# Ordering the first addition onto a chained weight chunk behind the low part of the chunk ahead, in a two-layer hybrid encoder on one core

## The chip, the core and the metric

The program runs on one core of a Trainium2 chip. TensorE multiplies matrices, VectorE and ScalarE do elementwise work, GpSimd does a little of it and issues transfers that add into their destination, SyncE issues the other transfers, and 16 DMA engines move the data. Each engine executes its instructions in the order in which the program lists them; an instruction that waits holds up all that are listed behind it on that engine. The metric is the device time of one execution in microseconds, and less is better.

## The reference, cut to what matters

Two layers, each a mixer and a gated feed-forward block with a residual addition, on 256 positions of 2048 channels in float32. The change lies in the feed-forward block:

```python
D_MODEL = 2048; SEQ = 256; DEPTH = 2; D_FF = 5632

def conv_ffn(x, w_up, conv_w, conv_b, w_down):
    u = x @ w_up
    up = jnp.pad(u, ((0, 0), (1, 1), (0, 0)))
    c = conv_w.astype(u.dtype)
    u = c[0] * up[:, :-2] + c[1] * up[:, 1:-1] + c[2] * up[:, 2:] + conv_b.astype(u.dtype)
    gate, val = jnp.split(u, 2, axis=-1)
    return (jax.nn.silu(gate) * val) @ w_down

def reference(x, ...):
    for layer in range(DEPTH):
        h = rms_norm(x, norm_mix[layer])
        ...
        x = x + mixed
        x = x + conv_ffn(rms_norm(x, norm_ffn[layer]), w_up[layer], conv_w[layer], conv_b[layer], w_down[layer])
    return x
```

Layer 0 mixes with pooling and grouped-query attention, layer 1 with a bidirectional matrix memory (mLSTM).

## The kernel before

**Weights as a stream.** All weights pass through one list of 870 chunks of 128 x 1024 float32 elements (a few are narrower), in the order in which TensorE uses them. `Stream` takes care of a chunk in three steps. `load` (L95) has SyncE fetch it into a tile `w`, of which there are six. `split` (L116) makes two halves of precision of it in a tile `hl`, of which there are four: ScalarE rounds it to the matmul's type (the high part, L127), and VectorE subtracts that from the original (the low part, L128). TensorE then computes with each chunk three products: high by high, high by low, low by high (all of its matmuls are recorded at L256). `next` (L145) hands the chunk over, and `ahead` (L133) has by then listed the loads five chunks further on and the splits two chunks further on. A tile `hl` is free for the rounding of chunk i when TensorE has finished chunk i - 4.

**The feed-forward block.** The 5632 hidden channels are worked through in six groups (FCH: 4, 8, 8, 8, 8, 8 tiles of 128). For a tile, `up` (L972) multiplies four chunks into the gate and value parts (64 matmuls); then ScalarE copies (L419), VectorE adds (L420) and scales (L976), ScalarE scales six times for the convolution (L981 to L983), VectorE adds twice (L984, L985), ScalarE applies SiLU (L989), VectorE multiplies (L990), and the result is split like a weight (L991, L992). Between the tiles of one group stand the down-projections of the group before.

**The seven-product scheme of the down-projection.** Part of the down-projection (both halves of the output columns for groups 2 to 4 in layer 0 and 1 to 4 in layer 1, one half for the earlier ones) is done with seven products of blocks instead of eight. It needs sums of activations (`combine`, L994) and sums of weights. A unit of kind "A" multiplies with four products for each pair of tiles: one chunk holds the weights of two of them, the next chunk those of the other two. For the second half of the output columns (h = 1) the weight sums are made as the chunks arrive, with two kinds of chunk that always come in pairs:

- a *sum chunk* (class `Sum`): `prepare` (L110) has SyncE load one part (L112) and GpSimd add the other onto it by an adding transfer (L113), into a tile `sum`, of which there are three; it is listed up to ten chunks ahead;
- a *chained chunk* (class `Chain`) right behind it: after its load, VectorE adds the sum chunk's first half onto its first half (L123), and then its first half onto its second half (L124). Only then can it be rounded.

There are 36 such pairs, 18 in each layer. In the groups that use the scheme for both halves of the columns a unit has two pairs (sum, chained, sum, chained), and it follows directly on the four chunks of an up-projection tile; the other groups have one pair at a time. Where the scheme is used for the first half of the columns (h = 0), the sums were made before in HBM by transfers alone (`premix`, L456), and no VectorE addition is needed.

**Who sets the order.** TensorE's instructions stand in the order of the text. For the other engines a scheduler at build time chooses the order on each engine: it simulates the program with durations of its own and takes, when an engine is free, an instruction whose inputs are ready by then. What is listed early in the text may be executed late, and the other way round. `reuse_waits` and the pools only decide when a tile may be written again. A dependence added by hand can have a semaphore behind it (`paced`, L452, uses such a one) or can bind the scheduler's order only.

Of the kernel before, what the change touches and what calls it, by code (L numbers as in the profile page):

```python
# [9 lines left out]
F32 = mybir.dt.float32  # L10
# [55 lines left out]
class Sum:  # L66


    def __init__(self, one, other):
        self.one, self.other = one, other  # L70
# [15 lines left out]
class Stream:  # L86


    def __init__(self, nc, wpool, spool, srcs, load_ahead, split_ahead):
        self.nc, self.wpool, self.spool, self.srcs = nc, wpool, spool, srcs  # L90
        self.la, self.sa = load_ahead, split_ahead
        self.w, self.hl = {}, {}
        self.n_load = self.n_split = self.at = 0
# [22 lines left out]
    def split(self, then=None):  # L116
        i = self.n_split
        w, n, width = self.w.pop(i)
        if isinstance(self.srcs[i], Sum):
            self.sum = w  # L120
        elif isinstance(self.srcs[i], Chain):
            half = CH * P // 2
            self.nc.vector.tensor_add(w[:, :half], w[:, :half], self.sum[:, :half])  # L123
            self.nc.vector.tensor_add(w[:, half:], w[:, half:], w[:, :half])  # L124
        hl = self.spool.tile([P, 2, CH * P], F32R, tag="hl", name=f"hl{i}")
        for c in range(0, width, n):
            (self.nc.vector.tensor_copy if i + c == 0 else self.nc.scalar.copy)(hl[:, 0, c : c + n], w[:, c : c + n])  # L127
            self.nc.vector.tensor_sub(hl[:, 1, c : c + n], w[:, c : c + n], hl[:, 0, c : c + n].bitcast(F32))  # L128
            then and then(c // n)
        self.hl[i] = hl  # L130
        self.n_split += 1

    def ahead(self, i, split=None):  # L133
        n = len(self.srcs)
        for j in range(self.n_load, min(n, i + 10)):
            if isinstance(self.srcs[j], Sum) and j not in self.w:
                self.prepare(j)
        while self.n_load < min(n, i + self.la + 1):
            if self.n_load >= self.n_split + self.la - self.sa + 1:
                self.split()  # L140
            self.load()
        while self.n_split < min(n, i + (self.sa if split is None else split) + 1):
            self.split()
# [64 lines left out]
def trunk(ctx: ExitStack, tc: tile.TileContext, gx, xT, xn, call, catt, cml, weights, mixes, out):  # L208
    nc = tc.nc
    v, a, g, pe = nc.vector, nc.scalar, nc.gpsimd, nc.tensor  # L210

    def pool(name, bufs, **kw):
        return ctx.enter_context(tc.tile_pool(name=name, bufs=bufs, **kw))
# [4 lines left out]
    wp = pool("wraw", 6)  # L218
    sp = pool("wsplit", 4)
# [7 lines left out]
    gcol = cp.tile([P, NG], F32, tag="gcol", name="gcol")  # L227
    a_x = actp.tile([P, KT, S], F32, tag="B1", name="xT")
    x = xp.tile([P, 2, D], F32, tag="x", name="x")
    st = Stream(nc, wp, sp, weights, 5, 2)  # L230

    gx0 = actp.tile([P, NG + 2 * S], F32, tag="B0", name="gx0")
    ctx.enter_context(tc.manual_schedule(engines={mybir.EngineType.PE}))
# [48 lines left out]
    class Norm:  # L282


        def __init__(self, n):
            self.n = n
            self.xx = actp.tile([P, KT, 2, S], F32R, tag="A", name=f"xx{n}")
            self.ss = smp.tile([P, 2, NB], F32, tag="nss", name=f"nss{n}")
            self.blocks, self.R, self.rcol = 0, None, None
# [1115 lines left out]
```

## Time and profile before

| | |
|---|---|
| three runs | 2172.79, 2177.34, 2180.11 us (median 2177.34) |
| the profiled execution | 2172.38 us, its span 2170.4 us |
| granted TensorE clock in it | 1.00 |
| TensorE matmul busy | 2160.9 us, 11424 instructions |
| VectorE busy | 1729.7 us, 2428 instructions |
| ScalarE busy | 1406.7 us, 2200 instructions |
| HBM read, written | 539.50 MB, 60.86 MB |

How to read the profile: all times are microseconds from the start of the span. PE is TensorE's matmul, PEld its loading of the stationary operand, DVE VectorE, ACT ScalarE, POOL GpSimd, SP SyncE (SPq is its queue, which issues transfers). In a row of the timeline stand the start, the duration, the engine, the line of the kernel, the operation, the tile written, an arrow, the tiles read, the shapes, and how many like instructions were merged; in brackets stands how long the engine was idle before it and what ended that. In a row that describes one line of the kernel stand the count, the shortest, median and longest duration in nanoseconds, and the first and last start; the rows under it give the engine's idle time ahead of that line in microseconds and the number of times, by what ended it. In a row of waits stand who waited for whom, the total, the number of times, and the longest.

### The profile page before, as it was taken

How to read it: one execution, taken by the hardware profiler on the slowest of the kernel's cores; microseconds unless marked ns; L12 is line 12 of the kernel's file. 1: busy time of each engine (PE TensorE's matmuls, PEld its weight loads, DVE VectorE, ACT ScalarE, POOL GpSimd, SP SyncE). 2: the span in 40 equal slices, each digit the busy share in tenths (PEclk: the TensorE clock that was granted, in tenths of full speed). 3: DMA queues.
4: the chain of work that ended last, by engine and by line, in shares of the span. 5: the costliest groups of instructions: out<-in, count | busy, mean ns of one | idle time of the engine just before them, and what ended most of it. 6: DMA issues, size and time to landing. Idle time of an engine off the chain costs nothing.

```text
span 2170.4 us, 31559 instructions
## 1 busy us (share of the span) xinstructions
PE 2160.9 (100%) x11424; PEld 1845.4 (85%) x11424; DVE 1729.7 (80%) x2428; ACT 1406.7 (65%) x2200; POOL 128.7 (6%) x160
## 2 busy tenths in 40 slices
PE   9999999999999999999999999999999999999999
PEld 7888888888888888889888888888888888888887
DVE  7686678887988888976777676667888898988896
ACT  7665576766677767666554554457676777776763
POOL 0011010000000000000000010110000000000000
PEclk9999999999999999999999999999999999999999
DMA  9668988787988877757688888998978787887774
GB/s 326 220 204 255 287 247 263 231 268 243 293 272 278 281 247 234 253 193 226 203 250 248 252 243 243 276 274 249 270 214 283 253 272 248 264 266 242 233 252 163
DMA packets 157790, 543.72 MB, mean 251 GB/s; under 512 B 17498, under 2 KB 19842, under 8 KB 157634
## 3 DMA queue, kind: packets, MB, share of 16 engines
q1 hardware_dynamic: 129056, 460.10, 61.1%
q0 software_dynamic: 17440, 48.51, 13.5%
q10 hardware_dynamic: 11138, 33.11, 4.6%
q8 instruction: 89, 1.46, 0.3%
q14 instruction: 67, 0.55, 0.1%
HBM read 539.50 MB, written 60.86 MB: 277 GB/s over the span
## 4 chain that ended last, share of the span: by engine, by line
PE 92%; DVE 4%; DMA 3%; issue 1%; ACT 1%; DVEq 0%; ACTq 0%; POOLq 0%
PE up L256 40%; PE pp L256 11%; PE op L256 8%; PE dn L256 6%; PE mv L256 4%; PE mq L256 4%; PE mk L256 4%; PE mo L256 4%; PE qproj L256 3%; DVE hl L128 2%; DMA w<-in_dn 1%; PE kproj L256 1%; PE vproj L256 1%; DMA sum<-in_dn 1%; PE pool L256 1%
## 5 line engine op out<-in xcount | busy, mean ns | idle before, releaser
L128 DVE TENSOR_TENSOR hl<-w,hl 128x1024 fp32r<-128x1024 f32 (+2 forms) x836 | 1002.8, 1211 | 223.3 <-ACT hl L127 220.6
L127 ACT CAST hl<-w 128x1024 fp32r<-128x1024 f32 (+2 forms) x835 | 857.2, 1043 | 450.5 <-PE up L256 134.3
L256 PE MATMUL up<-xx,hl 128*128 128x512 f32 (+1 forms) x5632 | 996.6, 337 | 3.2 <-DVE hl L128 3.0
L256 PEld LDWEIGHTS up<-xx,hl 128*128 128x128 f32 x5632 | 865.9, 188 | 137.9 <-DVE hl L128 7.9
L256 PE MATMUL pp<-hl,s 128*128 128x512 f32 x768 | 193.2, 393 | 0.4 <-DVE hl L128 0.4
L256 PEld LDWEIGHTS pp<-hl,s 128*128 128x128 f32 x768 | 141.3, 188 | 30.2 <-DVE hl L128 1.6
L256 PE MATMUL pp<-hl,g 128*128 128x512 f32 x576 | 147.9, 391 | 0.0
L419 ACT COPY tb_up<-up 128x512 f32<-128x512 f32 x88 | 51.6, 586 | 113.0 <-PE up L256 112.8
L256 PEld LDWEIGHTS pp<-hl,g 128*128 128x128 f32 x576 | 105.4, 188 | 20.7
L256 PE MATMUL dn<-hl,g 128*128 128x512 f32 x528 | 122.7, 390 | 0.0
L256 PEld LDWEIGHTS dn<-hl,g 128*128 128x128 f32 x528 | 98.7, 188 | 20.3
L983 ACT ACTIVATE y<-tb_up,cst 128x256 f32<-128x256 f32 x176 | 103.6, 589 | 0.0
L984 DVE TENSOR_TENSOR y<-y,z 128x510 f32<-128x510 f32 x88 | 60.5, 688 | 50.2 <-ACT y L983 50.2
L981 ACT ACTIVATE z<-tb_up,cst 128x256 f32<-128x256 f32 x176 | 88.4, 502 | 7.9 <-DVE tb_up L976 6.4
L256 PE MATMUL mk<-xx,hl 128*128 128x512 f32 (+1 forms) x512 | 92.1, 337 | 0.0
L256 PE MATMUL mq<-xx,hl 128*128 128x512 f32 (+1 forms) x512 | 92.1, 337 | 0.0
L256 PE MATMUL mv<-hl,xx 128*128 128x512 f32 (+2 forms) x480 | 91.7, 350 | 0.0
L256 PE MATMUL op<-hl,cat 128*128 128x512 f32 x384 | 91.6, 393 | 0.0
L420 DVE TENSOR_TENSOR tb_up<-up,tb_up 128x512 f32<-128x512 f32 x88 | 60.6, 688 | 38.4 <-ACT tb_up L419 38.4
L256 PE MATMUL mo<-hl,xx 128*128 128x512 f32 x384 | 90.5, 391 | 0.0
L256 PE MATMUL op<-hl,mcat 128*128 128x512 f32 x384 | 89.5, 392 | 0.0
L256 PEld LDWEIGHTS mq<-xx,hl 128*128 128x128 f32 x512 | 79.2, 188 | 11.6
(232 smaller groups left out, 2097.0 us busy)
## 6 DMA issues: line engine op xcount, KB each, us to landing
w<-in_up SPq DMA_DIRECT2D x352, 512.0 KB, 4.8
w<-in_dn SPq DMA_DIRECT2D x176, 512.0 KB, 4.5
w<-in_m_in SPq DMA_DIRECT2D x124, 512.0 KB, 5.3
m<-in_dn ACTq DMA_DIRECT2D x56, 512.0 KB, 6.0
w<-m SPq DMA_DIRECT2D x56, 512.0 KB, 4.8
w<-in_a_in SPq DMA_DIRECT2D x46, 512.0 KB, 4.8
sum<-in_dn SPq DMA_DIRECT2D x36, 512.0 KB, 4.9
sum<-in_dn POOLq DMA_DIRECT2D x36, 512.0 KB, 8.9
```

The lines of the kernel that those rows point to most:

```text
L127: (self.nc.vector.tensor_copy if i + c == 0 else self.nc.scalar.copy)(hl[:, 0, c : c + n], w[:, c : c + n])
L128: self.nc.vector.tensor_sub(hl[:, 1, c : c + n], w[:, c : c + n], hl[:, 0, c : c + n].bitcast(F32))
L256: last_mm[0] = pe.matmul(out_, lhsT, rhs, start=start, stop=stop, skip_group_check=True)
L419: a.copy(tb, ps[:, :, 1, :])
L420: v.tensor_add(tb, ps[:, :, 0, :], tb)
L981: a.activation(z[:, 0, j, :], u[:, j, :], AF.Copy, scale=cw(tl, 0))
L983: a.activation(y[:, j, :], u[:, j, :], AF.Identity, scale=cw(tl, 1), bias=cw(tl, 3))
L984: v.tensor_add(y[:, :, 1:S], y[:, :, 1:S], z[:, 0, :, 0 : S - 1])
```

## The change

`Stream` is given a function `behind`, and `split` remembers the last low part that it listed (`self.low`). The first addition onto a chained chunk gets a dependence on that low part, which is the one of the sum chunk just ahead. The dependence is of the kind that binds order only: both instructions are on VectorE, and no semaphore is waited for.

```diff
-    def __init__(self, nc, wpool, spool, srcs, load_ahead, split_ahead):
-        self.nc, self.wpool, self.spool, self.srcs = nc, wpool, spool, srcs
+    def __init__(self, nc, behind, wpool, spool, srcs, load_ahead, split_ahead):
+        self.nc, self.behind, self.wpool, self.spool, self.srcs = nc, behind, wpool, spool, srcs
...
         elif isinstance(self.srcs[i], Chain):
             half = CH * P // 2
-            self.nc.vector.tensor_add(w[:, :half], w[:, :half], self.sum[:, :half])
+            self.behind(self.nc.vector.tensor_add(w[:, :half], w[:, :half], self.sum[:, :half]), self.low)
             self.nc.vector.tensor_add(w[:, half:], w[:, half:], w[:, :half])
         hl = self.spool.tile([P, 2, CH * P], F32R, tag="hl", name=f"hl{i}")
         for c in range(0, width, n):
             (self.nc.vector.tensor_copy if i + c == 0 else self.nc.scalar.copy)(hl[:, 0, c : c + n], w[:, c : c + n])
-            self.nc.vector.tensor_sub(hl[:, 1, c : c + n], w[:, c : c + n], hl[:, 0, c : c + n].bitcast(F32))
+            self.low = self.nc.vector.tensor_sub(
+                hl[:, 1, c : c + n], w[:, c : c + n], hl[:, 0, c : c + n].bitcast(F32))
             then and then(c // n)
...
-    st = Stream(nc, wp, sp, weights, 5, 2)
+    order = mybir.DependencyInfo(mybir.DependencyClass.NoSync, mybir.DependencyReason.SCHED_ONLY)
+
+    def behind(ins, other):
+
+        tc.add_manual_dep(ins.ins, other.ins.name, order, reason="order")
+
+    st = Stream(nc, behind, wp, sp, weights, 5, 2)
```

## The prediction

> **What bounds the kernel now.** I read the page's engine totals first, then what the moved addition waited for, then VectorE and TensorE side by side where that wait is longest.
>
> ```profile
> span 2170.4 us, 31559 instructions
> PE 2160.9 (100%) x11424; PEld 1845.4 (85%) x11424; DVE 1729.7 (80%) x2428; ACT 1406.7 (65%) x2200; POOL 128.7 (6%) x160
> ```
>
> TensorE has 2170.4 - 2160.9 = 9.5 us without a matmul in it. No order of VectorE can give more than that, and part of it lies before the first weights arrive. So the gain has a ceiling and the loss has none.
>
> ```profile
> L123 DVE TENSOR_TENSOR w<-w,sum x36: 677/692/694, 298.3 to 2015.9; 128x512 f32<-128x512 f32 x36
>   DMA w<-in_dn: 26.2, 17
>   DMA sum<-in_dn: 4.2, 2
> L128 DVE TENSOR_TENSOR hl<-sum,hl x36: 1212/1217/1226, 310.6 to 2022.4; 128x1024 fp32r<-128x1024 f32 x36
> ```
>
> The first addition (L123) runs 36 times, and VectorE stood idle 26.2 + 4.2 = 30.4 us ahead of it for a transfer. The low part of the sum chunk ahead (L128 hl<-sum) starts later than its addition: 12.3 us in the first pair, 6.5 us in the last. The schedule has pulled the additions far forward, and VectorE, which runs in order, stops there with ready work behind.
>
> VectorE at the longest such wait in the first feed-forward layer:
>
> ```profile
> 668.76 0.69 DVE L123 TENSOR_TENSOR w<-w,sum 128x512 f32<-128x512 f32 x1 [1.90 <-DMA w<-in_dn]
> 669.37 0.68 DVE L420 TENSOR_TENSOR tb_up<-up,tb_up 128x512 f32<-128x512 f32 x1
> 669.97 0.68 DVE L124 TENSOR_TENSOR w<-w 128x512 f32<-128x512 f32 x1
> 670.57 0.68 DVE L976 TENSOR_TENSOR tb_up<-tb_up,R 128x512 f32<-128x512 f32 x1
> 671.18 2.35 DVE L128 TENSOR_TENSOR hl<-w,hl 128x1024 fp32r<-128x1024 f32 x2
> ...
> 679.32 1.21 DVE L128 TENSOR_TENSOR hl<-sum,hl 128x1024 fp32r<-128x1024 f32 x1
> ```
>
> The low part at 671.18 belongs to the up-projection chunk that TensorE wants next. Both additions and the idle 1.90 us stand ahead of it; the sum chunk's own low part is 10 us away. TensorE at this place and at three like it in the second layer:
>
> ```profile
> 671.25 0.61 PE L256 MATMUL up<-xx,hl 128*128 128x512 f32 x2
> 672.44 10.95 PE L256 MATMUL up<-xx,hl 128*128 128x256 f32 x62 [0.58 <-DVE hl L128]
> 1737.12 0.61 PE L256 MATMUL up<-xx,hl 128*128 128x512 f32 x2
> 1738.43 0.97 PE L256 MATMUL up<-xx,hl 128*128 128x256 f32 x4 [0.69 <-DVE hl L128]
> 1866.46 0.61 PE L256 MATMUL up<-xx,hl 128*128 128x512 f32 x2
> 1867.68 1.67 PE L256 MATMUL up<-xx,hl 128*128 128x256 f32 x8 [0.61 <-DVE hl L128]
> 1994.92 0.61 PE L256 MATMUL up<-xx,hl 128*128 128x512 f32 x2
> 1995.78 1.44 PE L256 MATMUL up<-xx,hl 128*128 128x256 f32 x7 [0.25 <-DVE hl L128]
> ```
>
> **What it removes.** No instruction is added or removed: the dependence is one of order on one engine and makes nothing wait on the chip. Both additions move (the second needs the first) from well ahead of the sum chunk's low part to behind it. At the four places the third matmul should start two matmul steps after the first. A step is 0.23 us (below), so 0.46; it starts 1.19, 1.31, 1.22 and 0.86 us after. Lost: 0.73 + 0.85 + 0.76 + 0.40 = 2.7 us. With additions and idle time gone from in front, the low part at 671.18 can start 1.90 + 2 x 0.60 us sooner, so I take these 2.7 us as won. Of the 30.4 us of idle VectorE most buys nothing, since TensorE did not stop there.
>
> **What it adds: a longer chain for each chained chunk.** Today both additions are done long before ScalarE rounds the chunk (L127). Afterwards the rounding must wait for: low part of the sum chunk, two additions, rounding, low part of the chained chunk. Whether that holds TensorE up is read in the first unit of the same block (two sum chunks, each followed by its chained chunk; rows of TensorE, VectorE, ScalarE):
>
> ```profile
> 683.24 2.24 PE L256 MATMUL pp<-hl,s 128*128 128x512 f32 x9
> 685.31 0.85 PE L256 MATMUL pp<-hl,g 128*128 128x512 f32 x3
> 686.00 2.22 PE L256 MATMUL pp<-hl,s 128*128 128x512 f32 x9
> ...
> 688.76 1.44 PE L256 MATMUL up<-xx,hl 128*128 128x512 f32 x7
> ```
> ```profile
> 682.78 1.21 DVE L128 TENSOR_TENSOR hl<-sum,hl 128x1024 fp32r<-128x1024 f32 x1
> 683.92 0.41 DVE L990 TENSOR_TENSOR s<-s,y 128x256 f32<-128x256 f32 x1
> 684.25 0.68 DVE L420 TENSOR_TENSOR tb_up<-up,tb_up 128x512 f32<-128x512 f32 x1
> ...
> 685.19 1.21 DVE L128 TENSOR_TENSOR hl<-w,hl 128x1024 fp32r<-128x1024 f32 x1
> 686.32 0.68 DVE L976 TENSOR_TENSOR tb_up<-tb_up,R 128x512 f32<-128x512 f32 x1
> ...
> 687.13 1.21 DVE L128 TENSOR_TENSOR hl<-w,hl 128x1024 fp32r<-128x1024 f32 x1
> ```
> ```profile
> 680.65 1.05 ACT L127 CAST hl<-sum 128x1024 fp32r<-128x1024 f32 x1 [1.73 <-PE up L256]
> ...
> 683.92 2.00 ACT L127 CAST hl<-w 128x1024 fp32r<-128x1024 f32 x2
> ```
>
> Twelve matmuls take 686.00 - 683.24 = 2.76 us: the step of 0.23 us, and 1.38 us for each chunk of six. The second sum chunk is used from 686.00, the second chained chunk from 687.38, its low part from the second matmul, 687.61. The rounding of the second sum chunk cannot start before 680.65, because TensorE held the buffer until then. From there, with nothing between: rounded at 681.70; low part from 681.70, the next VectorE instruction 1.14 us later (682.78 to 683.92), 682.84; first addition 0.69, second 0.68, done 684.21; rounding 1.05, 685.26; low part 1.21, 686.47. That is 1.1 us in time. Today this low part is done at 686.40, so the chain costs nothing if VectorE serves it at once.
>
> It does not quite. L990, L420 and one more short instruction stand behind the sum chunk's low part today: 685.19 - 683.92 = 1.27 us. What fits into the 1.05 us of rounding is free; what falls between the additions is not. The two extremes are 0 and 1.27 us of delay against 1.1 us in hand; and the next chunk's rounding queues behind this one on ScalarE, with its own use at 688.76. I take 0.2 us lost per unit, nearer the lower end since the rounding hides most of them. There are 14 such units (three blocks in layer 0 and four in layer 1, two each): 2.8 us. The eight chained chunks that come one to a slot are followed by down-projection or up-projection chunks of twice the length, and I cost them at nothing.
>
> One stall of this kind exists already:
>
> ```profile
> 575.66 0.74 PE L256 MATMUL pp<-hl,s 128*128 128x512 f32 x2 [0.41 <-DVE hl L128]
> ```
>
> Here an addition had waited for its sum in the same unit; without that wait these 0.4 us should go.
>
> **What hangs on the release of buffers.** SyncE issues loads in order, each when VectorE frees a buffer:
>
> ```profile
> 680.55 0.33 SPq L112 DMA_DIRECT2D sum<-in_dn  x1
> 682.89 0.33 SPq L107 DMA_DIRECT2D w<-in_dn  x1
> ```
>
> The first follows the sum chunk's low part (679.32 + 1.21 = 680.53), the second the chained chunk's. Afterwards the sum tile is held by the first addition too, 0.6 us longer, and the chained chunk's tile by as much as its low part is late, 0 to 1.3 us. GpSimd's adding transfer queues behind the same load. I take nothing, since the waits at L123 show the transfers late for the early additions rather than for the low parts; without that cover each late load costs those 0.6 to 1.3 us at the next up-projection chunk.
>
> [...] The two additions, dependent on one another, are exposed in the new chain. The rows above show L420, L124 and L976 starting 0.60 us apart with 0.68 us each, so one VectorE instruction begins before the end of the one ahead. [...]
>
> **The sum**, against the profiled execution (2172.38 us, of which 2170.4 are its span): -2.7 - 0.4 + 2.8 = -0.3 us. That execution lies 5 us (0.2%) below the runs' median of 2177.34, so I predict 2177 us. A difference under 0.3% (6.5 us) is about what a measurement of this kernel cannot tell from none.
>
> **Rivals.** (a) *All stalls go.* If VectorE, rid of 30 us of waiting, stays ahead everywhere, TensorE loses almost nothing:
>
> ```profile
> PEld up L256 <- DVE hl L128: 7.9, 13, 1.1
> PEld pp L256 <- DVE hl L128: 1.6, 4, 0.8
> ```
>
> These are the weight loads' waits for low parts, 7.9 + 1.6 = 9.5 us. A load runs ahead of its matmul, so less reaches the matmuls: more than the 3.1 us shown above and less than 9.5. With an estimate of 7 us the time would be 2170 us. For it: the waits vanish by construction. Against it: late loads (no addition near) cause some of these, and the chain is new. Chance 0.14.
>
> (b) *Slower: ScalarE's order turns over.* The up-projection's six scalings (L981 to L983) stand behind the roundings of the next up-projection chunks today:
>
> ```profile
> 688.58 0.50 ACT L981 ACTIVATE z<-tb_up,cst 128x256 f32<-128x256 f32 x1
> ...
> 691.10 0.59 ACT L983 ACTIVATE y<-tb_up,cst 128x256 f32<-128x256 f32 x1
> 691.59 1.03 ACT L127 CAST hl<-w 128x1024 fp32r<-128x1024 f32 x1
> ```
>
> They took 691.59 - 688.58 = 3.0 us with one small rounding among them. They are ready once L976 is done. If the chained rounding, now waiting for two additions, is placed so late that they are ready first, the schedule puts them ahead of the next chunk's rounding; that chunk has 0.9 us to pay with (low part done at 687.13 + 1.21 = 688.3, read by the third matmul at 688.76 + 0.46 = 689.2). Loss 3.0 - 0.9 = 2.1 us per unit, 29 us in all 14: 2206 us; in half of them 2192. It decides from the point where L976 ends before the second addition. For it: the second addition would end about 684.2, only 2 us ahead of L976's start. Against it: L976 stands behind the chained low part (685.19) today. Chance 0.20.
>
> (c) *The chain is late by one more thing*: two or three foreign instructions between additions, or loads late by 1 us in each unit. Loss 0.8 us per unit, 11 us: 2188 us. Chance 0.14. [...]
>
> (d) *It does not do what it says*: the additions stay where a transfer is late and wait again. All 36 stand on the other side now, so the order must move; time unchanged. Chance 0.02.
>
> **The numbers.** No change 0.50, its own range 2171 to 2184; (a) 0.14, (b) 0.20, (c) 0.14, (d) 0.02. Faster 0.14, same 0.50 + 0.02 = 0.52, slower 0.34. The range for 8 in 10 goes from 2170, the ceiling of the gain, to 2200; outside it are about half of (b) and some of (a).
>
> **What would show it.** Right: L123 behind every hl<-sum row, its idle time near 0, the stalls at the four places gone, PE's busy time within 4 us of before, and ScalarE's rounding of the chained chunk now ended by VectorE's L124. Wrong toward (b): the scalings ahead of the rounding that follows the chained chunk, and idle TensorE at that up-projection. Wrong toward (c): idle TensorE inside pp rows. Wrong altogether: new stalls outside the feed-forward layers, where no addition is.

## The result, and the profile after

| | before | after |
|---|---|---|
| runs beside each other | 2172.79 to 2180.11 us, median 2178.24 (4) | 2193.08 to 2194.12 us, median 2193.73 (4) |
| the profiled execution | 2172.38 us, span 2170.4 | 2193.08 us, span 2191.3 |
| granted TensorE clock in it | 1.000 | 0.997 |

The ratio is 1.0075, with a 95% interval of 1.0056 to 1.0094: the change makes the kernel slower by about 0.75%. The time lies inside the range of the prediction, but the forecast, "no change", is wrong.

The page of after, its span and its busy times:

```profile
span 2191.3 us, 31590 instructions
...
PE 2168.9 (99%) x11424; PEld 1851.9 (85%) x11424; DVE 1737.5 (79%) x2428; ACT 1405.1 (64%) x2200; POOL 128.4 (6%) x160
```

TensorE stands without a matmul for 2191.3 - 2168.9 = 22.4 us instead of 9.5, and its matmuls, as many as before, take 8.0 us longer. Those two, 12.9 + 8.0 = 20.9 us, are the whole difference of the spans.

**The 12.9 us.** The waits of TensorE in after (who waited for whom, us in total, times, longest):

```profile
PE pp L263 <- ACT hl L127: 11.0, 7, 1.7
PE pp L263 <- DVE hl L128: 5.3, 7, 0.8
```

Before, the same view has two rows for the weight chunks, `PE up L256 <- DVE hl L128` with 3.0 us in six places and `PE pp L256 <- DVE hl L128` with 0.4 us in one. These are gone and 16.3 us are new: 16.3 - 3.4 = 12.9. The new ones are not spread over fourteen units: seven places wait twice each, first for ScalarE's rounding, then for VectorE's low part.

The two additions, by line (duration shortest, median and longest in ns, first and last start; below it who waited):

```profile
L123 DVE TENSOR_TENSOR w<-w,sum x36: 681/685/687, 310.7 to 2043.8; 128x512 f32<-128x512 f32 x36
```
```profile
L124 DVE TENSOR_TENSOR w<-w x36: 682/685/694, 311.6 to 2044.5; 128x512 f32<-128x512 f32 x36
...
  ACT hl L127: 22.4, 30
```

Under L123 the list of what VectorE sat idle for is empty, where 30.4 us of transfers stood before: the order did move, at all 36. In its place ScalarE now waits 22.4 us for the second addition. TensorE at the place of the first quoted stall of before, and then in the first unit of that block:

```profile
674.17 11.30 PE L263 MATMUL up<-xx,hl 128*128 128x512 f32 x64
...
688.08 1.54 PE L263 MATMUL pp<-hl,s 128*128 128x512 f32 x6
691.30 0.50 PE L263 MATMUL pp<-hl,s 128*128 128x512 f32 x1 [1.68 <-ACT hl L127]
692.56 1.22 PE L263 MATMUL pp<-hl,s 128*128 128x512 f32 x2 [0.76 <-DVE hl L128]
```

The stall at the first up-projection chunk is gone: 64 matmuls run without a break. The second sum chunk starts at 688.08, so the second chained chunk is wanted at 688.08 + 1.38 = 689.46. Its first matmul starts at 691.30, 1.84 us late, and the second, which needs the low part, 1.26 us behind it instead of 0.23, 1.03 us late: 2.9 us in all. ScalarE and VectorE behind this:

```profile
684.20 1.06 ACT L127 CAST hl<-w 128x1024 fp32r<-128x1024 f32 x1 [0.84 <-DVE w L124]
685.15 1.04 ACT L127 CAST hl<-sum 128x1024 fp32r<-128x1024 f32 x1
...
690.20 3.88 ACT L127 CAST hl<-w 128x1024 fp32r<-128x1024 f32 x4 [2.91 <-issue]
693.99 0.51 ACT L988 ACTIVATE z<-tb_up,cst 128x256 f32<-128x256 f32 x1
```
```profile
681.90 0.69 DVE L123 TENSOR_TENSOR w<-w,sum 128x512 f32<-128x512 f32 x1
682.50 0.42 DVE L997 TENSOR_TENSOR s<-s,y 128x256 f32<-128x256 f32 x1
682.84 0.68 DVE L1068 TENSOR_TENSOR x<-x,pp 128x512 f32<-128x512 f32 x1
683.44 0.69 DVE L124 TENSOR_TENSOR w<-w 128x512 f32<-128x512 f32 x1
...
686.43 1.22 DVE L128 TENSOR_TENSOR hl<-sum,hl 128x1024 fp32r<-128x1024 f32 x1
687.57 0.68 DVE L123 TENSOR_TENSOR w<-w,sum 128x512 f32<-128x512 f32 x1
688.17 0.68 DVE L427 TENSOR_TENSOR tb_up<-up,tb_up 128x512 f32<-128x512 f32 x1
688.77 0.75 DVE L1012 TENSOR_TENSOR s<-sf,s 128x384 fp32r<-128x384 f32 x2
689.44 0.68 DVE L124 TENSOR_TENSOR w<-w 128x512 f32<-128x512 f32 x1
690.04 0.68 DVE L983 TENSOR_TENSOR tb_up<-tb_up,R 128x512 f32<-128x512 f32 x1
691.28 2.36 DVE L128 TENSOR_TENSOR hl<-w,hl 128x1024 fp32r<-128x1024 f32 x2 [0.55 <-ACT hl L127]
```

Read it backwards. The low part at 691.28 waits for the rounding at 690.20, that for the second addition at 689.44. Between the two additions three foreign instructions (L427, two of L1012) take 689.44 - 688.17 = 1.27 us. The first addition stands behind the second sum chunk's low part (686.43), and that chunk's rounding, at 685.15, stands on ScalarE right behind the first chained chunk's, which has itself waited 0.84 us for its own second addition. So the chain of the first chained chunk is followed by the chain of the second. The second sum chunk's rounding starts 688.08 - 685.15 = 2.9 us ahead of its use; before it was 686.00 - 680.65 = 5.35 us. The four roundings at 690.20 come ahead of the scalings (693.99).

**The 8.0 us.** Stretches of 3.40 us behind each of the seven waits (the stretch, its length, busy time and number of instructions of PE, PEld, DVE, ACT and POOL, the granted TensorE clock, the transfers' share and GB/s):

```profile
563.50:566.90 3.40, 3.40 (x22) 2.96 (x21) 2.56 (x4) 3.40 (x7) 0.85 (x1) 1.00 1.07 308
692.60:696.00 3.40, 3.40 (x9) 2.72 (x10) 3.31 (x3) 3.40 (x7) 0.86 (x1) 0.51 0.95 239
825.70:829.10 3.40, 3.40 (x12) 2.82 (x11) 2.59 (x4) 3.40 (x8) 0.00 (x0) 0.50 0.95 271
1637.40:1640.80 3.40, 3.40 (x22) 2.96 (x21) 2.55 (x4) 3.40 (x8) 0.61 (x1) 1.00 1.00 304
1767.80:1771.20 3.40, 3.40 (x12) 2.81 (x11) 2.60 (x4) 3.40 (x8) 0.85 (x1) 0.51 0.91 280
1900.30:1903.70 3.40, 3.40 (x20) 2.93 (x19) 2.59 (x3) 3.40 (x8) 0.65 (x1) 1.00 0.95 324
2030.60:2034.00 3.40, 3.40 (x11) 2.75 (x10) 2.93 (x3) 3.40 (x8) 0.00 (x0) 0.50 0.71 219
```

Behind four of the seven waits TensorE gets half the clock for about one such stretch and does about half the matmuls in it. That is 3.40 x (0.49 + 0.50 + 0.49 + 0.50) = 6.7 us of the 8.0; the rest is not placed.

### The profile page after: what moved, and what is told of

It reads as the page before. It is cut to its first block, busy times and chain, and to the rows that moved or that the text cites. A ratio compares the mean times of both kernels' runs of the same rounds, so it can differ in the third digit from the quotient of the medians.

```text
span 2191.3 us, 31590 instructions
## 1 busy us (share of the span) xinstructions
PE 2168.9 (99%) x11424; PEld 1851.9 (85%) x11424; DVE 1737.5 (79%) x2428; ACT 1405.1 (64%) x2200; POOL 128.4 (6%) x160
## 4 chain that ended last, share of the span: by engine, by line
PE 92%; DVE 4%; issue 2%; ACT 2%; ACTq 0%; DVEq 0%
PE up L263 41%; PE pp L263 12%; PE op L263 8%; PE dn L263 5%; PE mv L263 4%; PE mq L263 4%; PE mk L263 4%; PE mo L263 4%; PE qproj L263 3%; DVE hl L128 2%; PE kproj L263 1%; PE vproj L263 1%; PE pool L263 1%; ACT hl L127 1%; PE qk L263 1%
## 5 line engine op out<-in xcount | busy, mean ns | idle before, releaser
L128 DVE TENSOR_TENSOR hl<-w,hl 128x1024 fp32r<-128x1024 f32 (+2 forms) x836 | 1000.7, 1212 | 234.3 <-ACT hl L127 231.4
L127 ACT CAST hl<-w 128x1024 fp32r<-128x1024 f32 (+2 forms) x835 | 853.6, 1043 | 456.7 <-PE up L263 131.7
L263 PE MATMUL up<-xx,hl 128*128 128x512 f32 (+1 forms) x5632 | 998.5, 338 | 0.3
L263 PEld LDWEIGHTS up<-xx,hl 128*128 128x128 f32 x5632 | 870.6, 189 | 133.0 <-DVE hl L128 1.6
L263 PE MATMUL pp<-hl,s 128*128 128x512 f32 x768 | 197.5, 396 | 16.3 <-ACT hl L127 11.0
L263 PEld LDWEIGHTS pp<-hl,s 128*128 128x128 f32 x768 | 141.0, 188 | 50.1 <-ACT hl L127 14.0
L263 PE MATMUL pp<-hl,g 128*128 128x512 f32 x576 | 149.9, 395 | 0.0
L263 PEld LDWEIGHTS pp<-hl,g 128*128 128x128 f32 x576 | 106.4, 189 | 21.0
L263 PE MATMUL dn<-hl,g 128*128 128x512 f32 x528 | 122.7, 390 | 0.0
L263 PEld LDWEIGHTS dn<-hl,g 128*128 128x128 f32 x528 | 98.7, 188 | 20.4
L427 DVE TENSOR_TENSOR tb_up<-up,tb_up 128x512 f32<-128x512 f32 x88 | 60.6, 689 | 44.4 <-ACT tb_up L426 44.3
L263 PE MATMUL mk<-xx,hl 128*128 128x512 f32 (+1 forms) x512 | 92.1, 337 | 0.0
L263 PE MATMUL mq<-xx,hl 128*128 128x512 f32 (+1 forms) x512 | 92.1, 337 | 0.0
L263 PE MATMUL mv<-hl,xx 128*128 128x512 f32 (+2 forms) x480 | 91.7, 350 | 0.0
L263 PE MATMUL op<-hl,cat 128*128 128x512 f32 x384 | 91.6, 393 | 0.0
L263 PE MATMUL mo<-hl,xx 128*128 128x512 f32 x384 | 90.5, 391 | 0.0
L263 PE MATMUL op<-hl,mcat 128*128 128x512 f32 x384 | 89.5, 392 | 0.0
L263 PEld LDWEIGHTS mq<-xx,hl 128*128 128x128 f32 x512 | 79.2, 188 | 11.6
```

The source lines that it names most:

```text
L128: self.low = self.nc.vector.tensor_sub(hl[:, 1, c : c + n], w[:, c : c + n], hl[:, 0, c : c + n].bitcast(F32))
L263: last_mm[0] = pe.matmul(out_, lhsT, rhs, start=start, stop=stop, skip_group_check=True)
L427: v.tensor_add(tb, ps[:, :, 0, :], tb)
```

## The experiments

There are 36 chained chunks in order of use: eight that come one to a slot, and 28 in fourteen units of two. The seven blocks with double units have two units each, here the first and the second. The first theory was that the second chained chunk's own order, seven edges of the 36, costs the time. Against it stood that VectorE is too full at this place, that the lateness comes through ScalarE from the chunk ahead, and, beside these, that the clock takes a share of its own. Unless a ratio stands, a time is that of one run; where one stands, the time is a median and the span and the rows are those of the one profiled run. Each stands beside a median of before of 2175.0 (the first, second, third and fifth run below), 2175.5 (the fourth, sixth, seventh and eighth) or 2175.2 us (the last three).

### The second chained chunk of each first unit left free

```diff
-            self.behind(self.nc.vector.tensor_add(w[:, :half], w[:, :half], self.sum[:, :half]), self.low)
+            first = self.nc.vector.tensor_add(w[:, :half], w[:, :half], self.sum[:, :half])
+            if self.chained not in SECOND:          # (7, 11, 15, 21, 25, 29, 33)
+                self.behind(first, self.low)
+            self.chained += 1
```

> Of the 36 first additions, the seven on the second chained chunk of the first unit of each double block are free again (as before); the other 29 stay ordered behind the low part. Theory A (the loss is the long chain sum chunk - chained chunk - sum chunk - chained chunk through VectorE and ScalarE in that unit alone): TensorE no longer waits 1.85 + 1.03 us there, its clock stays at 1.0, and the stalls at the up-projection chunk ahead of that unit stay away as in the changed kernel; span 2164 to 2169 us, 2 to 6 us under the kernel before. Theory B (every addition that is ordered costs about the same, wherever it stands: 20.9 us over 36): 29/36 of the loss stays, span about 2187 us. Theory C (the additions are harmless where they stand, VectorE's whole order was shaken up by the edge): no sure number, but new stalls at other places, span over 2175 us.

Measured 2181.86 us, ratio 1.0032 (1.0019 to 1.0044), span 2178.2, clock 1.0 (0.998 and 0.999 in three of the six runs). TensorE's waits:

```profile
PE pp L269 <- DVE hl L134: 4.9, 7, 1.5
```

The numbers of theories A and B both fail; what comes is what C named, new stalls and a span over 2175 us. The seven double waits are gone, and so is the halved clock in the profiled run, but TensorE now waits for the first chained chunk of the unit (five of the seven waits), and for 2.3 us in five places at up-projection chunks. ScalarE ahead of one such wait:

```profile
686.28 0.59 ACT L432 COPY tb_up<-up 128x512 f32<-128x512 f32 x1 [0.73 <-PE up L269]
686.76 1.05 ACT L133 CAST hl<-w 128x1024 fp32r<-128x1024 f32 x1
```

The chunk's second addition ended on VectorE at 685.71 (it starts at 685.02 and takes 0.69). Its rounding starts at 686.76, 1.05 us later, behind a copy that had waited 0.73 us for TensorE. So the edges that were left cost too, in another form, and here again through ScalarE's order.

### Only these seven ordered

```diff
-            if self.chained not in SECOND:
+            if self.chained in SECOND:
```

> The reverse: only those seven additions are ordered behind the low part, the other 29 are free. Theory A with the whole chain of four chunks needed: the rounding of the second sum chunk is no longer held behind the rounding of the first chained one, so TensorE loses 0 to 1 us per unit; the stalls at the up-projection chunk ahead remain (about 3 us in all); span 2170 to 2178 us. Theory A' (the second chained chunk's own additions are enough): 2.9 us in each of seven units and lowered clock in some, span 2190 to 2197 us. Theory B: 7/36 of the loss, span about 2175 us.

Measured 2197.38 us, span 2195.5, clock 0.998: slow as the first theory has it, and yet not for its reason. VectorE in the first unit of a block:

```profile
822.04 0.69 DVE L130 TENSOR_TENSOR w<-w 128x512 f32<-128x512 f32 x1
...
823.41 0.69 DVE L126 TENSOR_TENSOR w<-w,sum 128x512 f32<-128x512 f32 x1 [0.48 <-DMA w<-in_dn]
...
824.83 0.69 DVE L130 TENSOR_TENSOR w<-w 128x512 f32<-128x512 f32 x1
825.43 3.49 DVE L134 TENSOR_TENSOR hl<-w,hl 128x1024 fp32r<-128x1024 f32 x3
```

The chained chunk's second addition is done by 822.73 and could be rounded at once. But the next chunk's additions, free and early, stand ahead of its low part (825.43) and one of them waits 0.48 us for a transfer; in six of the seven first units the next chunk's addition waits so, for 0.37 to 2.17 us. This is the old fault at a new place. A time near the expected one can still come from another cause.

### One addition in place of two

The two dependent additions become one of double width, which adds the sum's first half onto both halves of the chained chunk; the chained chunk's own first half is not added onto its second.

```diff
-            self.behind(self.nc.vector.tensor_add(w[:, :half], w[:, :half], self.sum[:, :half]), self.low)
-            self.nc.vector.tensor_add(w[:, half:], w[:, half:], w[:, :half])
+            w2 = w.rearrange("p (a b) -> p a b", a=2)
+            once = self.sum[:, : CH * P // 2].unsqueeze(1).to_broadcast([P, 2, CH * P // 2])
+            self.behind(self.nc.vector.tensor_add(w2, w2, once), self.low)
```

> The two dependent additions of 128x512 become one of 128x1024 that adds the sum chunk's first half to both halves (the chained chunk's own first half is not added onto its second half); it is ordered as in the changed kernel. VectorE's work is about the same, but nothing can come between. Theory A, with the foreign instructions between the two additions as a main part of the chain (0.9 us in the first pair, 1.3 us in the second): the wait of 2.9 us per unit falls to 0.3 to 1.0 us, the clock stays at 1.0; span 2165 to 2173 us. If what counts is only that the addition stands behind the low part: span 2188 to 2193 us, as with the change.

Measured 2176.24 us, span 2174.4, clock 1.0. TensorE's waits, and the second chained chunk's addition in the first unit of a block with what follows:

```profile
PE pp L263 <- DVE hl L128: 6.5, 7, 1.0
```
```profile
814.88 1.22 DVE L124 TENSOR_TENSOR w<-w,sum 128x1024 f32<-128x1024 f32 x1
816.01 0.42 DVE L999 TENSOR_TENSOR g<-s,g 128x256 fp32r<-128x256 f32 x1
```

The one addition takes VectorE 1.13 us to the next start. Two that follow one another directly take 0.72 + 0.60 = 1.32 us (in after 574.29, 575.01 and, for the next instruction, 575.62). The work is nearly the same, only nothing can be placed between its halves. By the starts of the matmuls a first unit loses 1.23 us instead of 2.9. So 1.7 us of the 2.9 hang on the place between the two additions, in both chained chunks together; 1.2 us do not. The rest is larger than expected.

### The order bound to the low part two chunks ahead

```diff
-            self.behind(..., self.low)
+            self.behind(..., self.lows[-2])
...
-            self.low = self.nc.vector.tensor_sub(...)
+            self.lows.append(self.nc.vector.tensor_sub(...))
```

> Each first addition is ordered behind the low part two chunks ahead instead of one (for the second chained chunk of a unit: behind the first one's low part). Theory A as it stands now (what is late is the second addition and the rounding behind it, with foreign instructions in between; the sum chunk's low part is just one link): the second addition still comes late in the first units, most of the 2.9 us per unit stays, span 2180 to 2190 us. Rival (only the edge onto the sum chunk's own low part hurts): the loss is gone, span 2164 to 2172 us.

Measured 2190.03 us, span 2188.0, clock 0.997, near the upper end of what was expected. `PE pp L263 <- ACT hl L127` still has 7.4 us in six places and `<- DVE hl L128` 5.0 in seven. One chunk of freedom (1.4 us) does not open the chain.

### The wait filled with matmuls by zeros

Eight matmuls with a weight tile of zeros are added into the running sum ahead of the second chained chunk's products, in the first unit of each block.

```diff
+            none = kp.tile([P, P], F32R, tag="none", name=f"none{layer}")
+            v.tensor_scalar_mul(none, ident, 0.0)
...
+                    if kind == "A" and h == 1 and js == (0, 1) and m == 6:
+                        for _ in range(8):
+                            pe.matmul(pss[e], none, norm.xx[:, 0].rearrange("p a b -> p (a b)"), start=False,
+                                      stop=False, skip_group_check=True)
```

> The changed kernel with eight matmuls of 128x512 by a tile of zeros (1.84 us, they add nothing to the result) ahead of the second chained chunk's products in the first unit, where TensorE waits 1.85 us. Theory D (the granted clock falls to one half for 3.4 us because TensorE is idle for most of a stretch): with the wait filled the clock stays at 1.0 in all seven units, and the 4 x 1.7 = 6.8 us come back; span 2183 to 2187 us. Rival (the lowered clock has nothing to do with the idle time): four such stretches stay, span 2190 to 2196 us.

Measured 2190.0 us, span 2188.2. The granted clock is 1.0 throughout. TensorE in the unit shown above, and its waits:

```profile
689.11 1.54 PE L263 MATMUL pp<-hl,s 128*128 128x512 f32 x6
690.49 2.00 PE L1054 MATMUL pp<-xx,none 128*128 128x512 f32 x8
692.35 0.49 PE L263 MATMUL pp<-hl,s 128*128 128x512 f32 x1
693.61 0.74 PE L263 MATMUL pp<-hl,s 128*128 128x512 f32 x2 [0.77 <-DVE hl L128]
```
```profile
PE pp L263 <- DVE hl L128: 6.0, 13, 0.8
```

The second chained chunk starts 1.86 us behind the end of the sum chunk's six steps, and the low part is late as in after, so the fillers hardly cost anything of their own. With the idle time the four halved stretches are gone too: by this one execution they come from the idle time, not from the change itself. But the span is only 2191.3 - 2188.2 = 3.1 us shorter, not 6.7. Thirteen places wait now instead of seven: the second units begin to lose time too, about 0.45 us each by the starts of their matmuls, and they do so as well in the three blocks whose clock was not halved in after. What differs there is the order on VectorE: in all seven second units L427 now stands between the two additions of the second chained chunk (574.49, 575.09, 575.69: 1.20 us from one addition to the other), where in after they are neighbours (574.29 and 575.01: 0.72 us). These 7 x 0.45 = 3.2 us are most of the 3.6 us that are missing, and they come from the order that the scheduler chose with the fillers, not from the clock.

### All 36 bound to the low part five chunks ahead

```diff
-            self.behind(..., self.lows[-2])
+            self.behind(..., self.lows[-5])
```

> Each first addition is ordered behind the low part five chunks ahead; for the first chained chunk of a unit that is the first up-projection chunk, at which TensorE stood still before. Theory A: the additions still end some chunks ahead of the rounding, so there is no chain; the stalls of 0.3 to 0.95 us at that up-projection chunk (five in the kernel before, 3.5 us) go; span 2164 to 2168 us, 2 to 6 us under the kernel before. Rival (every edge costs by itself, since it takes freedom from the schedule): span over 2172 us.

Measured 2173.67 us, ratio 0.9991 (0.9982 to 1.0000), span 2173.0, some 5 us over the first expectation. By its number it is the rival that holds, that every edge costs by itself; the next run, with 29 edges fewer and the same time, speaks against it. The double waits are gone. The profiled run has one large stop left, at a chunk that comes one to a slot, where an addition waited 4.63 us for its transfer:

```profile
1522.11 0.69 DVE L123 TENSOR_TENSOR w<-w,sum 128x512 f32<-128x512 f32 x1 [4.63 <-DMA w<-in_dn]
```
```profile
1525.80 6.42 PE L263 MATMUL up<-xx,hl 128*128 128x256 f32 x27 [2.29 <-DVE hl L128]
```

### Only the first chained chunk of each first unit bound, five chunks ahead

```diff
...
+            if self.chained in FIRST:               # (6, 10, 14, 20, 24, 28, 32)
+                self.behind(first, self.lows[-5])
```

> Only the seven first additions on the first chained chunk of each double block are ordered, behind the low part five chunks ahead; the other 29 are free. Theory A: the same stalls go as with all 36, span 2164 to 2169 us. If the gain of the change came from the other 29 as well (fewer waits for transfers there), the span stays at 2168 to 2171 us.

Measured 2173.70 us, ratio 0.9991 (0.9982 to 0.9999), span 2171.4, just above both ranges expected: the seven edges alone bring as much as all 36.

### The first units freed, the second left as in the change

```diff
...
+            if self.chained not in SECOND:
+                self.behind(first, self.lows[-5 if self.chained in FIRST else -1])
```

> The same seven behind the low part five chunks ahead, the second pair of the first units free, and the remaining 22 (second units and single pairs) as in the changed kernel, right behind the sum chunk's low part. Theory A (only in the first unit of a double block, where VectorE is full, is the chain too long): no more loss than with the seven alone, span 2164 to 2170 us. Rival (the chain costs in second units too and was hidden there by the longer time of the first units): 0.3 to 0.6 us in each of seven second units, span 2168 to 2174 us.

Measured 2175.99 us, ratio 1.0003 (0.9993 to 1.0012). A second unit:

```profile
837.06 1.76 PE L270 MATMUL pp<-hl,s 128*128 128x512 f32 x7
839.53 0.74 PE L270 MATMUL pp<-hl,s 128*128 128x512 f32 x2 [0.70 <-DVE hl L135]
```

The eighth matmul of the row should start seven steps of 0.23 us after the first, at 838.67, and starts at 839.53. By the starts of the chunks around them six of the seven second units lose 0.97 to 1.04 us each (the first one 3.3 us, by a double wait), where in after none loses over 0.14. So the order costs there as well, as the rival has it. By its 0.48 us the addition that is L427 in after, and L434 here, accounts for about half of it: it stands between the two additions in all seven (1.20 us from one to the other instead of 0.72). That the first unit's stop, just ahead of them, hides the other half in after is argued, not shown.

### Five ahead in the double units, one ahead in the single slots

```diff
...
+            self.behind(first, self.lows[-1 if self.chained in SINGLE else -5])   # (0, 1, 2, 3, 4, 5, 18, 19)
```

> The 28 additions of the double blocks are ordered behind the low part five chunks ahead, the eight of single pairs behind the sum chunk's own low part (one ahead), as in the changed kernel. With all 36 five ahead TensorE stood still for 4.1 us once, at a single pair whose addition waited 4.6 us for a transfer, and its clock was halved for 3.4 us after it. Theory: single pairs have slack for the chain, so that stop goes and nothing new comes; span 2166 to 2169 us, some 5 us under the one with all 36. Rival (that stop is a transfer's lateness and comes back at the rounding): span 2171 to 2174 us.

Measured 2172.86 us, ratio 0.9990 (0.9981 to 0.9999), span 2169.5, just above what was expected; the spans of all eleven runs go from 2168.8 to 2173.9, with a median of 2170.9. TensorE's longest group of waits for weights, and VectorE's idle time ahead of the first addition for the chained chunk's transfer (26.2 us before):

```profile
PE up L268 <- DVE hl L133: 1.5, 5, 0.5
```
```profile
  DMA w<-in_dn: 8.7, 7
```

In the profiled run it halves the waits at the up-projection (3.0 us before) and leaves 0.5 us in the units. But the 5 us that it was to gain on the version with all 36 do not come: 0.9990 and 0.9991 with intervals that cover one another, and median spans of 2170.9 and 2171.7 us. The stop at the single slot, seen in one execution there, was no steady loss of that size. The three versions, with all 36, seven or these 28 additions bound five chunks ahead, are not told apart. The whole gain is 0.1%, which fits the ceiling of 9.5 us read from the page of before.

### VectorE relieved: four additions of the down-projection left out

The additions that drain the down-projection of the earlier half (`drain`, kind B with h = 0) are left out.

```diff
-                    else:
+                    elif kind == "A" or h == 1:
```

> The changed kernel without the four VectorE additions that bring the products of a unit of kind B, first half of the columns, onto x and acc (that part of the down-projection is left out of the sum); they stand on VectorE 2.4 us long in five of the seven first units. If VectorE's fullness ahead of the first pair is what makes the chain late: the wait in these five units falls from 2.9 us to under 1 us and the clock stays up; span 2168 to 2178 us. If the length of the chain alone does it: the wait stays over 2 us, span 2183 to 2190 us.

Measured 2180.43 us, span 2178.7. By the starts of the matmuls, the five first units that had these additions ahead of them lose 0.60 us instead of 2.9 and their second units 0.49. (In these second units L427 again stands between the two additions; in the two other second units it does not, and they lose nothing.) TensorE's waits:

```profile
PE pp L263 <- DVE hl L128: 4.2, 12, 0.8
PE pp L263 <- ACT hl L127: 2.6, 2, 1.7
```

Of the seven waits for a rounding two are left. In after, one of the left-out additions stands between the two additions of the first chained chunk (L1068 at 682.84) and more of them stand ahead, so the theory of the full VectorE holds for these five units. The two others, the first double unit of each layer, had none of them and keep their double wait; what fills VectorE there was not tried.

### The first chained chunk of each first unit freed, all others as in the change

```diff
...
+            self.behind(first, self.lows[-5 if self.chained in FIRST else -1])
```

> The changed kernel with one difference: the seven additions on the first chained chunk of a double block are ordered behind the low part five chunks ahead, so they are early; the second pair keeps the order behind its sum chunk's low part. If the second sum chunk's rounding was late because ScalarE held it behind the first chained chunk's rounding (it started 2.5 us after TensorE had freed the buffer): it now starts on time, the wait in the first units falls from 2.9 us to about 1 us as in the second units, no halved clock; span 2174 to 2180 us. Rival (the second pair's own chain is the whole loss): 2.9 us per first unit stay, span 2185 to 2191 us.

Measured 2176.65 us, span 2174.8, clock 1.0. ScalarE and TensorE in a first unit:

```profile
810.00 1.05 ACT L132 CAST hl<-sum 128x1024 fp32r<-128x1024 f32 x1 [1.42 <-issue]
```
```profile
815.32 1.76 PE L268 MATMUL pp<-hl,s 128*128 128x512 f32 x7
```

The second sum chunk's rounding starts 815.32 - 810.00 = 5.3 us ahead of its use again, as in before, and a first unit loses 0.3 to 0.8 us instead of 2.9, although the second chained chunk's own order is untouched. So 2.1 us of the 2.9, in most of them, come from the chain of the chunk ahead. How much of that is the place in ScalarE's queue, and how much the two additions that leave VectorE at this point, these runs do not separate. The second units lose 0.5 to 1.1 us, as when the first units were freed altogether.

## Why the prediction was right and wrong

**What it removes: right.** The first addition stands behind its sum's low part at all 36, VectorE's 30.4 us of waiting there are gone, and so are the four stalls at the first up-projection chunk (2.7 us predicted). TensorE's waits before, 3.0 + 0.4 us, vanish with them. That most of the 30.4 us would buy nothing was right too.

**What it adds: the size is wrong by the whole result.** The step that failed is "The rounding of the second sum chunk cannot start before 680.65 ... From there, with nothing between". It let that rounding start when TensorE releases the buffer. In the changed kernel it stands on ScalarE behind the first chained chunk's rounding, which waits for its own additions; it lost 2.4 us of its lead (5.35 to 2.9 us), and with these the 1.1 us in hand were gone before the second chain began. The prediction looked at the chunk that queues behind the chained rounding, not at the one queued behind the chained chunk before it. The sum closes in the unit shown: 1.1 us in hand, less 2.4 us of lead, less 1.5 us by which the chain from that rounding to the last low part is longer than the 5.8 us predicted (685.15 to 692.50 is 7.35 us), makes 2.8 us late, and 2.9 were lost. Freeing the chunk ahead alone brought the lead back and the loss down to 0.3 to 0.8 us.

**"I take 0.2 us lost per unit"** fell with it. The prediction gave the foreign instructions between 0 and 1.27 us and took the low end, "since the rounding hides most of them". The schedule put exactly 1.27 us of them between the two additions of the second chained chunk, where the rounding hides nothing, and joining the additions took 1.7 us off the loss. The 2.8 us over fourteen units became 2.9 us in seven, 2.0 in one of them, with at most 0.14 in the other seven; in the variants without the first unit's stop those lose about 1 us, about half of it by an instruction placed between their additions.

**The clock was no term of the sum.** It took 6.7 us, about a third of the 20.9, and by it the sign "PE's busy time within 4 us of before" failed too (8.0 us).

**The rivals.** (b) did not come: the scalings follow the next roundings (693.99), though L983 stands directly behind the second addition. (c) names the right kind, "two or three foreign instructions between additions", and idle TensorE inside pp rows was its sign; its estimate of 0.8 us per unit was too small for the first units (2.9 us) and its 14 units too many. (a) needed VectorE to stay ahead everywhere. That the time lies inside the range, which reached 2200 us for the sake of (b), is luck as far as the mechanism goes. That one VectorE instruction begins before the end of the one ahead holds in after too: an instruction starts 0.60 us behind one that takes 0.69 (681.90, 682.50). The second addition, which needs the first, starts 0.72 us behind it where nothing stands between (574.29, 575.01).

**Loads.** "I take nothing" for tiles held longer cannot be judged alone; no wait for a transfer is left at the additions of after.

## What to carry to other kernels

An order that removes a wait on one engine can lengthen the chain through the others. Follow it for at least two chunks in a row, because the second can inherit the lateness of the first on an engine that they share, here ScalarE, where the second rounding lost 2.4 us of its lead. Between two dependent instructions on a full engine count every instruction that the schedule may put there at its full price (here three, 1.27 us). And when work runs too early, bound how early it may be (five chunks ahead here) instead of tying it to its last possible moment; the seven edges did as much as 36.

## What was not expected of the hardware

In after the four halved stretches stand on one grid of time. They begin at 692.55, 825.67, 1767.75 and 2030.58 (read from the granted clock in windows of 0.05 us) and last 3.41 us each. From one start to the next it is 133.12, 942.08 and 262.83 us, which is 39, 276 and 77 times 3.413 us (133.12 / 39). Two slots of that grid, counted from these starts, the first followed by the full clock and the second by half of it (columns as above):

```profile
559.43:562.84 3.41, 1.88 (x7) 1.35 (x8) 2.90 (x4) 3.41 (x4) 0.00 (x0) 1.00 1.02 217
822.26:825.67 3.41, 1.43 (x5) 0.98 (x6) 2.85 (x4) 3.29 (x4) 0.00 (x0) 1.00 0.74 135
```

TensorE was busy for 0.98, 1.43, 1.35 and 0.98 us in the four slots ahead of the halved stretches, and for 1.88 us or more in every other slot between the first and the last matmul. So the waits were hit here whose idle time fell mostly into one slot, and the three were spared whose idle time was split between two: the one of 2.0 us at 1637 and two of 2.9 us. Idle times of 1.68 and 0.76 us with one matmul between them stand ahead of the halved stretch at 692.55 (from 689.62 and 691.80) and, equally long, ahead of a wait that was spared (from 1896.11 and 1898.30). This is read from seven waits of one execution. Whether the busy time of a slot decides, and from what figure on, is not shown: no slot there was busy for between 1.43 and 1.88 us.

On VectorE an addition that reads what the instruction just ahead wrote starts 0.72 us behind it (in all seven second units of after), where one that does not need it starts 0.60 us behind (687.57, 688.17); each takes 0.68 to 0.69 us.
